# The top-256 selection of a sparse-attention decoder: its number built in float bits, blocks 2 and 3 counted on ScalarE as well

## The chip, the cores and the metric

The kernel runs on one core of a Trainium2 chip. Its time is the device time of one launch in microseconds (us). Four engines compute, each with its own queue worked off in order: TensorE (PE in the profile; PEld is its weight load), VectorE (DVE), ScalarE (ACT) and GpSimd (POOL); SyncE (SP) issues the DMAs. They meet only at semaphores.

## The reference

Two layers of a decoder over 1024 tokens of 1024 features. The first mixer is a sparse attention in which an indexer scores every earlier key for every query and the 256 best keys are kept; the second is a sliding-window attention. Each layer also reads a small memory and ends in a gated MLP with a causal convolution. The part that matters here:

```python
dots  = jnp.einsum('bqhd,bsd->bqhs', qi, k_idx)               # 16 index heads
score = jnp.einsum('bqhs,bqh->bqs', relu(dots), wi)
score = jnp.where(causal[None], score, -jnp.inf)
_, idx = lax.top_k(score, 256)                                # per query, of up to 1024 keys
# softmax attention of 8 heads over the keys in idx alone
```

## The kernel before

Activations lie with the features on the partitions and 512 tokens (a half) in a row. A product in float32 is made of three passes in the reduced-precision format (`mm3`, lines 256 to 258): every operand is split into a high part, which ACT casts, and a rest, which POOL or DVE subtracts. Weights are split ahead of their use (cast on line 99, ACT; rest on line 100, POOL; two units ahead), products are evacuated from PSUM by ACT and then DVE (lines 264 and 265). PSUM has two buffers `pS` of 1024 columns and four `pB` of 512.

The queries are worked in blocks of 128. Block b has (b + 1) * 128 keys. `indexer` makes the scores: for each of 16 heads PE multiplies into one or two `pB` (line 1188), ACT takes the relu of each piece (line 1191), and DVE adds head by head into the block's `work` tile (line 1194 for the first head, 1196 for the others). `topk` then finds the 256th largest score of every row, for several blocks at once: 32 steps, one for each bit of a float32. In each step every block is counted against its candidate `cand`: a block on DVE by a comparison with an accumulator (line 1224, tile `hit`), a block in the argument `act` by a Sign pass with an accumulator on ACT (line 1232, tile `sign`). Small DVE instructions on tiles of 128x2 or 128x4 (lines 1229, 1246, 1249 to 1253) keep or drop the bit and make the next candidate. Blocks on ACT are refined at the end by four passes over the row and a fresh count (lines 1263 to 1272), since a Sign pass counts ties by half. Masks follow (lines 1280 to 1290).

The order of each queue is that in which the program issues, and that is set by `tick`: PE's work in the foreground calls it with an estimate in ns, and background generators (the indexer, `topk`, norms, the memory's attention) run as far as that budget goes. A `yield` names what a step costs, so `pace` (1400 ns a count for blocks 2 and 3, 2400 ns for blocks 4 to 7) spaces the counts. In the program of `index`, blocks 2 and 3 are scored, then selected, while blocks 4 to 7 are scored; then blocks 4 to 7 are selected, with blocks 6 and 7 on ACT, through the attention and the first MLP.

Of the kernel before, what the change touches and what calls it, by code (L numbers as in the profile page):

```python
# [17 lines left out]
F32 = mybir.dt.float32  # L18
R32 = mybir.dt.float32r
I32 = mybir.dt.int32  # L20
BF16 = mybir.dt.bfloat16
AF = mybir.ActivationFunctionType
OP = mybir.AluOpType
# [7 lines left out]
TOPK = 256  # L31
# [142 lines left out]
class Trunk:  # L174
# [1028 lines left out]
    def topk(self, blks, pace, act=()):  # L1203

        nc, nb = self.nc, len(blks)
        wks = [self.work[b][:, :(b + 1) * 128] for b in blks]
        ints = self.sb.tile([128, 6, 4], I32, name="ti", tag="ti", bufs=2)
        found, flip, cand, keep, less, pick = [ints[:, i, :nb] for i in range(6)]
        floats = self.sb.tile([128, 5, 4], F32, name="tc", tag="tc", bufs=2)
        cnt, need, reach, low, high = [floats[:, i, :nb] for i in range(5)]
        order = [i for i in range(nb) if blks[i] not in act]
        order[1:1] = [i for i in range(nb) if blks[i] in act]

        def hits(tag):  # L1220
            return self.sb.tile([128, 1024], BF16, name=tag, tag=tag, bufs=1)

        def count(i, op):
            nc.vector.tensor_scalar(hits("hit")[:, :(blks[i] + 1) * 128], wks[i], cand[:, i:i + 1].bitcast(F32), 0.0,
                                    op0=op, op1=OP.add, accum_out=cnt[:, i:i + 1])

        def counts():
            if act:
                nc.vector.tensor_scalar(less, cand, -(1 << 31), None, op0=OP.bitwise_xor)
            for i in order:  # L1230
                if blks[i] in act:
                    nc.scalar.activation(hits("sign")[:, :(blks[i] + 1) * 128], wks[i], AF.Sign,
                                         bias=less[:, i:i + 1].bitcast(F32), accum_out=cnt[:, i:i + 1])
                else:
                    count(i, OP.is_ge)
                yield pace

        for i, b in enumerate(blks):
            nc.vector.memset(need[:, i:i + 1], float(2 * TOPK - 1 - (b + 1) * 128 if b in act else TOPK))
        nc.vector.memset(found, 0)  # L1240
        nc.vector.memset(cand, 0)
        yield from counts()
        nc.vector.tensor_tensor(reach, cnt, need, op=OP.is_lt)
        nc.vector.tensor_scalar(flip, reach, -1.0, 0.0, op0=OP.mult, op1=OP.add)
        for bit in range(30, -1, -1):
            nc.vector.scalar_tensor_tensor(cand, found, 1 << bit, flip, op0=OP.bitwise_or, op1=OP.bitwise_xor)
            yield from counts()
            if act:
                nc.vector.tensor_tensor(reach, cnt, need, op=OP.is_ge)
                nc.vector.tensor_scalar(keep, reach, float(1 << bit), 0.0, op0=OP.mult, op1=OP.add)  # L1250
            else:
                nc.vector.tensor_scalar(keep, cnt, float(TOPK), float(1 << bit), op0=OP.is_ge, op1=OP.mult)
            nc.vector.tensor_tensor(found, found, keep, op=OP.bitwise_or)
        nc.vector.tensor_tensor(cand, found, flip, op=OP.bitwise_xor)
        for i in range(nb):
            count(i, OP.is_gt)
            yield pace
        for i, (b, wk) in enumerate(zip(blks, wks)):
            if b in act:
                c = cand[:, i:i + 1]  # L1260
                far = self.t4(1024)[:, :(b + 1) * 128]
                for end, side, away, near in ((low, OP.is_le, 3.4e38, OP.min), (high, OP.is_gt, -3.4e38, OP.max)):
                    nc.vector.tensor_scalar(far, wk, c.bitcast(F32), away, op0=side, op1=OP.mult)
                    yield 1.6 * (b + 1) * 128
                    nc.vector.tensor_tensor_reduce(far, far, wk, 1.0, away, op0=OP.add, op1=near,
                                                   accum_out=end[:, i:i + 1])
                    yield 1.6 * (b + 1) * 128
                lo, hi, p = low[:, i:i + 1].bitcast(I32), high[:, i:i + 1].bitcast(I32), pick[:, i:i + 1]
                nc.vector.tensor_scalar(p, cnt[:, i:i + 1], float(TOPK), -1.0, op0=OP.is_ge, op1=OP.mult)
                nc.vector.tensor_tensor(c, lo, hi, op=OP.bitwise_xor)  # L1270
                nc.vector.tensor_tensor(c, c, p, op=OP.bitwise_and)
                nc.vector.tensor_tensor(c, c, hi, op=OP.bitwise_xor)
                yield 1.6 * (b + 1) * 128
                count(i, OP.is_gt)
                yield 1.6 * (b + 1) * 128
        nc.vector.tensor_scalar(cnt, cnt, -1.0, float(TOPK), op0=OP.mult, op1=OP.add)
        for i, wk in enumerate(wks):
            n = (blks[i] + 1) * 128
            eq, rank = self.t4(1024)[:, :n], self.t4(1024)[:, :n]
            v = cand[:, i:i + 1].bitcast(F32)  # L1280
            nc.vector.tensor_scalar(eq, wk, v, 1.0, op0=OP.is_equal, op1=OP.mult)
            yield 0.8 * n
            nc.vector.tensor_tensor_scan(rank, eq, eq, 0.0, op0=OP.add, op1=OP.max)
            yield 2 * 0.8 * n
            nc.vector.scalar_tensor_tensor(rank, rank, cnt[:, i:i + 1], eq, op0=OP.is_le, op1=OP.mult)
            yield 2 * 0.8 * n
            nc.vector.scalar_tensor_tensor(wk, wk, v, rank, op0=OP.is_le, op1=OP.subtract)
            yield 2 * 0.8 * n
            nc.vector.tensor_scalar(wk, wk, NEG, 1.0, op0=OP.mult, op1=OP.mult)
            yield 0.8 * n  # L1290
# [395 lines left out]
    def run(self):  # L1686
        nc, a = self.nc, self.a
# [52 lines left out]
        def memory():  # L1740
            yield from self.mem_norm()
            yield from self.mem_kv(0)
            del self.mn
# [6 lines left out]
        def index():  # L1750
            yield 12864
            yield from self.indexer((2, 3))
            bt.append(self.add_bg(self.topk((2, 3), 1400)))
            while "qi1" not in self.marks:
                yield 500
            yield 9000
            be[1] = 0.65
            yield from self.indexer((4, 5, 6, 7))
            late.append(self.add_bg(self.topk((4, 5, 6, 7), 2400, (6, 7))))

        late = []
        bt = []
        be = self.add_bg(index(), 1.0)
        self.finish_bg(b1)
        del x1
# [29 lines left out]
        for hf in range(2):  # L1795
# [8 lines left out]
            if hf == 0:  # L1804
# [14 lines left out]
                bm, bt = self.add_bg(memory()), []  # L1819
            else:  # L1820
# [9 lines left out]
                def mem_kv():  # L1830
                    yield 120000
                    yield from self.mem_norm()
                    yield 3000
                    yield from self.mem_kv(1)
                    del self.mn

                bt = [self.add_bg(mem_kv(), 0.8)]
# [289 lines left out]
```

## Time and profile before

| | |
|---|---|
| median of 3 runs (2682.31 to 2684.56) | 2682.89 us |
| the profiled execution | 2683.7 us |
| its span, first to last instruction | 2681.9 us |
| mean granted PE clock | 0.965 |
| busy: PE, DVE, POOL, ACT | 92%, 66%, 50%, 44% |
| selection of blocks 2 and 3: first count and end of the last step | 184.5 and 357.8 us |
| selection of blocks 4 to 7: first and last Sign pass | 401.4 and 797.8 us |

PE is the busiest engine, and what it does is the same before and after; time moves where PE waits, or where its granted clock falls, which in the records is 1.2 GHz instead of 2.4 for some us after a wait. The two selections run in the stretch from 184 to 860 us, so that is the stretch to read, engine by engine.

### The profile page before, as it was taken

To read this page: it belongs to the slowest core of one execution; us is meant where nothing else is said; L and a number is where in the kernel's file an instruction comes from. 1 tells how busy PE (TensorE), PEld (TensorE's weight loads), DVE (VectorE), ACT (ScalarE), POOL (GpSimd) and SP (SyncE) were. 2 spreads that over 40 slices of the span, in tenths; PEclk is the share of its full clock that TensorE was granted. 3 is DMA by queue.
4 is the path that set the end of the run, shared out by engine and by line. 5 is a ranking of instruction groups with operands and counts; after the bars stand their busy time and mean duration, and the time that the engine had idled before them with its cause. 6 is when DMAs were issued, how large, how long until landed. Compare 5 with 4: busy or idle time off the path is not lost. (4 is left out here: it accounts for less than half of the span.)

```text
span 2681.9 us, 33704 instructions
## 1 busy us (share of the span) xinstructions
PE 2480.3 (92%) x11912; PEld 2066.6 (77%) x11912; DVE 1775.3 (66%) x3016; ACT 1190.1 (44%) x2214; POOL 1344.5 (50%) x942
## 2 busy tenths in 40 slices
PE   6789889988998999989999989999989999999997
PEld 5667667867776789877778878878867888887886
DVE  7899997876679556664663361588786565655446
ACT  4444456644442555433333333678744444442103
POOL 4544343444554643336756555656645666664203
PEclk8899999998998999999999999999999999999998
DMA  5444345422222254232323327453144323249301
GB/s 198 145 150 133 127 135 209 148 72 88 84 85 74 77 201 126 87 118 79 104 84 110 102 75 235 136 187 115 67 157 157 120 101 124 97 145 365 134 24 63
DMA packets 122233, 338.00 MB, mean 126 GB/s; under 512 B 13136, under 2 KB 30032, under 8 KB 122064
## 3 DMA queue, kind: packets, MB, share of 16 engines
q1 hardware_dynamic: 122064, 335.85, 37.4%
q8 instruction: 94, 1.54, 0.2%
q14 instruction: 75, 0.61, 0.1%
HBM read 262.40 MB, written 73.40 MB: 125 GB/s over the span
## 5 line engine op out<-in xcount | busy, mean ns | idle before, releaser
L100 POOL TENSOR_TENSOR t<-t,t 128x1024 fp32r<-128x1024 f32 (+1 forms) x292 | 720.6, 2483 | 483.1 <-ACT t L99 328.9
L256 PE MATMUL pB<-t,t 128*128 128x512 f32 (+3 forms) x1824 | 683.1, 375 | 12.0 <-DVE t L766 4.7
L257 PE MATMUL pB<-t,t 128*128 128x512 f32 (+3 forms) x1824 | 680.3, 373 | 11.6 <-DVE t L447 9.4
L258 PE MATMUL pB<-t,t 128*128 128x512 f32 (+3 forms) x1824 | 680.1, 373 | 8.9 <-POOL t L100 8.9
L256 PE MATMUL pS<-t,t 128*128 128x512 f32 (+1 forms) x1460 | 578.7, 396 | 59.5 <-DVE t L852 28.0
L258 PE MATMUL pS<-t,t 128*128 128x512 f32 (+1 forms) x1460 | 572.7, 392 | 13.1 <-POOL t L100 13.1
L257 PE MATMUL pS<-t,t 128*128 128x512 f32 (+1 forms) x1460 | 572.6, 392 | 0.8 <-DVE t L498 0.8
L256 PEld LDWEIGHTS pB<-t,t 128*128 128x128 f32 (+1 forms) x1824 | 347.0, 190 | 73.3 <-DVE t L766 5.0
L257 PEld LDWEIGHTS pB<-t,t 128*128 128x128 f32 (+1 forms) x1824 | 347.0, 190 | 71.9 <-DVE t L447 10.7
L258 PEld LDWEIGHTS pB<-t,t 128*128 128x128 f32 (+1 forms) x1824 | 346.9, 190 | 71.0 <-POOL t L100 10.8
L256 PEld LDWEIGHTS pS<-t,t 128*128 128x128 f32 x1460 | 284.1, 195 | 122.1 <-DVE t L852 37.7
L99 ACT CAST t<-t 128x1024 fp32r<-128x1024 f32 (+1 forms) x292 | 296.9, 1043 | 101.8 <-PE pS L258 44.4
L258 PEld LDWEIGHTS pS<-t,t 128*128 128x128 f32 x1460 | 283.3, 194 | 74.1 <-POOL t L100 17.5
L257 PEld LDWEIGHTS pS<-t,t 128*128 128x128 f32 x1460 | 284.0, 195 | 53.0 <-DVE t L498 1.6
L106 POOL TENSOR_TENSOR t<-t,t 128x512 fp32r<-128x512 f32 x133 | 177.4, 1347 | 136.9 <-ACT t L105 136.9
L265 DVE TENSOR_TENSOR t<-pB,t 128x512 fp32r<-128x512 f32 (+3 forms) x248 | 149.8, 623 | 84.3 <-ACT t L264 81.8
L264 ACT CAST t<-pB 128x512 fp32r<-128x512 f32 (+3 forms) x248 | 126.5, 535 | 151.8 <-PE pB L258 82.5
L1040 DVE TENSOR_TENSOR t<-t,pS 128x1024 f32<-128x1024 f32 (+1 forms) x92 | 108.0, 1174 | 124.0 <-PE pS L258 123.8
L796 POOL TENSOR_TENSOR t<-t,t 128x512 f32<-128x512 f32 x44 | 57.2, 1299 | 201.8 <-ACT t L795 201.8
L852 DVE TENSOR_TENSOR t<-t,pS 128x1024 f32<-128x1024 f32 x88 | 106.5, 1217 | 65.2 <-PE pS L258 65.0
L1415 POOL TENSOR_SCALAR t<-t,st 128x128 f32<-128x128 f32 (+3 forms) x64 | 47.9, 751 | 141.6 <-DVE st L1414 78.9
L787 ACT ACTIVATE t<-t,conv 128x512 f32<-128x512 f32 x44 | 35.9, 816 | 175.8 <-DVE t L786 175.8
(239 smaller groups left out, 3405.3 us busy)
## 6 DMA issues: line engine op xcount, KB each, us to landing
t<-in_up SPq DMA_DIRECT2D x138, 512.0 KB
t<-in_down SPq DMA_DIRECT2D x66, 512.0 KB
G_d<-t SPq DMA_DIRECT2D x44, 512.0 KB
t<-G_d SPq DMA_DIRECT2D x44, 512.0 KB
t<-in_a_in SPq DMA_DIRECT2D x42, 512.0 KB
t<-in_b_in SPq DMA_DIRECT2D x28, 512.0 KB
t<-in_a_out SPq DMA_DIRECT2D x20, 512.0 KB
t<-x_d SPq DMA_DIRECT2D x20, 512.0 KB
```

Of the source, the lines that this page charges most:

```text
L99: nc.scalar.copy(hi[:, :w], raw[:, :w])
L100: nc.gpsimd.tensor_tensor(lo[:, :w], raw[:, :w], hi[:, :w].bitcast(F32), op=OP.subtract)
L106: nc.gpsimd.tensor_tensor(hl[:, 1], src, hl[:, 0].bitcast(F32), op=OP.subtract)
L256: mm(out, a[0], b[0], start=start, stop=False, skip_group_check=again)
L257: mm(out, a[0], b[1], start=False, stop=False, skip_group_check=again)
L258: mm(out, a[1], b[0], start=False, stop=stop, skip_group_check=again)
L264: nc.scalar.copy(hi, src)
L265: nc.vector.tensor_tensor(lo, src, hi.bitcast(F32), op=OP.subtract)
L796: nc.gpsimd.tensor_tensor(v, v, rb[0], op=OP.mult)
L852: nc.vector.tensor_tensor(x[dp][:, :, t], x[dp][:, :, t], S, op=OP.add)
L1040: nc.vector.tensor_tensor(xp, xp, S, op=OP.add)
L1415: nc.gpsimd.tensor_scalar(Pt[:, :n], Pt[:, :n], st[:, 2:3], 1.0, op0=OP.mult, op1=OP.mult)
```

## The change

In `topk` the blocks are put in a new order, those counted on DVE (`own`) first. `cand` is now itself the number that is built: a step makes `drop`, the bit if too few scores reach the candidate, and takes it back and sets the next bit with one exclusive-or instruction. That is two small instructions for each group of blocks in a step, where there were three (no block on ACT) or five. For the group on ACT the number is kept with its sign bit turned over, so that it serves as the bias of the Sign pass. All Sign passes of a step have one width, that of the widest block; the narrower blocks' tiles are filled up by a memset on POOL. The Sign passes are issued first in a step, right behind the decision of the step before, and the `yield` for them comes behind the DVE counts. Blocks 2 and 3 are now both in `act`: they have no DVE count in the 32 steps, and are refined at the end as blocks 6 and 7 are.

```diff
--- before.py
+++ after.py
@@ -1208,14 +1208,19 @@
 
 
+
+
         nc, nb = self.nc, len(blks)
+        own = [b for b in blks if b not in act]
+        blks = own + [b for b in blks if b in act]
         wks = [self.work[b][:, :(b + 1) * 128] for b in blks]
-        ints = self.sb.tile([128, 6, 4], I32, name="ti", tag="ti", bufs=2)
-        found, flip, cand, keep, less, pick = [ints[:, i, :nb] for i in range(6)]
-        floats = self.sb.tile([128, 5, 4], F32, name="tc", tag="tc", bufs=2)
-        cnt, need, reach, low, high = [floats[:, i, :nb] for i in range(5)]
-        order = [i for i in range(nb) if blks[i] not in act]
-        order[1:1] = [i for i in range(nb) if blks[i] in act]
+        ints = self.sb.tile([128, 3, 4], I32, name="ti", tag="ti", bufs=2)
+        cand, drop, pick = [ints[:, i, :nb] for i in range(3)]
+        floats = self.sb.tile([128, 3, 4], F32, name="tc", tag="tc", bufs=2)
+        cnt, low, high = [floats[:, i, :nb] for i in range(3)]
+        wide = (max(act) + 1) * 128 if act else 0
+        parts = [(slice(0, len(own)), TOPK), (slice(len(own), nb), 2 * TOPK - 1 - wide)]
+        parts = [p for p in parts if p[0].stop > p[0].start]
 
         def hits(tag):
             return self.sb.tile([128, 1024], BF16, name=tag, tag=tag, bufs=1)
@@ -1224,34 +1229,29 @@
             nc.vector.tensor_scalar(hits("hit")[:, :(blks[i] + 1) * 128], wks[i], cand[:, i:i + 1].bitcast(F32), 0.0,
                                     op0=op, op1=OP.add, accum_out=cnt[:, i:i + 1])
 
-        def counts():
+        nc.vector.memset(cand, 0)
+        if act:
+            nc.vector.tensor_scalar(cand[:, len(own):], cand[:, len(own):], -(1 << 31), None, op0=OP.bitwise_xor)
+            for b in act:
+                if (b + 1) * 128 < wide:
+                    nc.gpsimd.memset(self.work[b][:, (b + 1) * 128:wide], -3e38)
+        for bit in range(31, -1, -1):
+            for b in act:
+                i = blks.index(b)
+                nc.scalar.activation(hits("sign")[:, :wide], self.work[b][:, :wide], AF.Sign,
+                                     bias=cand[:, i:i + 1].bitcast(F32), accum_out=cnt[:, i:i + 1])
+            for i in range(len(own)):
+                count(i, OP.is_ge)
+                yield pace
             if act:
-                nc.vector.tensor_scalar(less, cand, -(1 << 31), None, op0=OP.bitwise_xor)
-            for i in order:
-                if blks[i] in act:
-                    nc.scalar.activation(hits("sign")[:, :(blks[i] + 1) * 128], wks[i], AF.Sign,
-                                         bias=less[:, i:i + 1].bitcast(F32), accum_out=cnt[:, i:i + 1])
-                else:
-                    count(i, OP.is_ge)
-                yield pace
-
-        for i, b in enumerate(blks):
-            nc.vector.memset(need[:, i:i + 1], float(2 * TOPK - 1 - (b + 1) * 128 if b in act else TOPK))
-        nc.vector.memset(found, 0)
-        nc.vector.memset(cand, 0)
-        yield from counts()
-        nc.vector.tensor_tensor(reach, cnt, need, op=OP.is_lt)
-        nc.vector.tensor_scalar(flip, reach, -1.0, 0.0, op0=OP.mult, op1=OP.add)
-        for bit in range(30, -1, -1):
-            nc.vector.scalar_tensor_tensor(cand, found, 1 << bit, flip, op0=OP.bitwise_or, op1=OP.bitwise_xor)
-            yield from counts()
-            if act:
-                nc.vector.tensor_tensor(reach, cnt, need, op=OP.is_ge)
-                nc.vector.tensor_scalar(keep, reach, float(1 << bit), 0.0, op0=OP.mult, op1=OP.add)
-            else:
-                nc.vector.tensor_scalar(keep, cnt, float(TOPK), float(1 << bit), op0=OP.is_ge, op1=OP.mult)
-            nc.vector.tensor_tensor(found, found, keep, op=OP.bitwise_or)
-        nc.vector.tensor_tensor(cand, found, flip, op=OP.bitwise_xor)
+                yield pace * len(act)
+            for at, need in parts:
+                nc.vector.tensor_scalar(drop[:, at], cnt[:, at], float(need), float(1 << bit) if bit < 31 else -1.0,
+                                        op0=OP.is_lt, op1=OP.mult)
+                nc.vector.scalar_tensor_tensor(cand[:, at], drop[:, at], 1 << bit >> 1, cand[:, at],
+                                               op0=OP.bitwise_xor, op1=OP.bitwise_xor)
+        if act:
+            nc.vector.tensor_scalar(cand[:, len(own):], cand[:, len(own):], -(1 << 31), None, op0=OP.bitwise_xor)
         for i in range(nb):
             count(i, OP.is_gt)
             yield pace
@@ -1750,7 +1750,7 @@
         def index():
             yield 12864
             yield from self.indexer((2, 3))
-            bt.append(self.add_bg(self.topk((2, 3), 1400)))
+            bt.append(self.add_bg(self.topk((2, 3), 1400, (2, 3))))
             while "qi1" not in self.marks:
                 yield 500
             yield 9000
```

PE's and SP's queues hold the same instructions in the same order as before. Three places where the others differ:

First, ACT's queue where the selection of blocks 2 and 3 begins. L1191 with 128x512 are the last relus of block 3, L264 an evacuation, L466 the high part of the normed second half. Before:

```order
L1191 ACTIVATE t_1446<-pB 128x512
L1191 ACTIVATE t_1463<-pB 128x512
L1191 ACTIVATE t_1469<-pB 128x512
L264 CAST t_1493<-pS 128x1024
L99 CAST t_1500<-t_1207 128x1024
L466 CAST t_1510<-t_1386 128x1024
L466 CAST t_1514<-t_1455 128x1024
L99 CAST t_1522<-t_1333 128x1024
```

and with the change, where the line of the Sign pass is L1241:

```order
L1191 ACTIVATE t_1446<-pB 128x512
L1191 ACTIVATE t_1463<-pB 128x512
L1191 ACTIVATE t_1469<-pB 128x512
L1241 ACTIVATE sign,tc<-t_1110,ti 128x512
L1241 ACTIVATE sign,tc<-t_1297,ti 128x512
L264 CAST t_1494<-pS 128x1024
L99 CAST t_1501<-t_1207 128x1024
L466 CAST t_1511<-t_1386 128x1024
L466 CAST t_1515<-t_1455 128x1024
L99 CAST t_1523<-t_1333 128x1024
```

The first two Sign passes stand ahead of L264, L99 and both L466; they wait for the first `cand`, which is DVE's row behind L1200 of block 3.

Second, one step in the scoring of block 6 (pieces of 512 and 256 columns): ACT before, two heads and a weight cast,

```order
L1191 ACTIVATE t_2295<-pB 128x512
L1191 ACTIVATE t_2295<-pB 128x256
L1191 ACTIVATE t_2317<-pB 128x512
L1191 ACTIVATE t_2317<-pB 128x256
L99 CAST t_2328<-t_2037 128x1024
L1191 ACTIVATE t_2344<-pB 128x512
```

ACT with the change, the same heads,

```order
L1191 ACTIVATE t_2280<-pB 128x512
L1191 ACTIVATE t_2280<-pB 128x256
L1191 ACTIVATE t_2300<-pB 128x512
L1191 ACTIVATE t_2300<-pB 128x256
L1241 ACTIVATE sign,tc<-t_1110,ti 128x512
L1241 ACTIVATE sign,tc<-t_1297,ti 128x512
L99 CAST t_2312<-t_2025 128x1024
L1191 ACTIVATE t_2328<-pB 128x512
```

and DVE with the change, where L1249 and L1251 are the decision:

```order
L1196 SCALAR_TENSOR_TENSOR t_2251<-t_2280,wtok,t_2251 128x768
L1196 SCALAR_TENSOR_TENSOR t_2251<-t_2300,wtok,t_2251 128x768
L1249 TENSOR_SCALAR ti<-tc 128x2
L1251 SCALAR_TENSOR_TENSOR ti<-ti 128x2
L1196 SCALAR_TENSOR_TENSOR t_2251<-t_2328,wtok,t_2251 128x768
L1196 SCALAR_TENSOR_TENSOR t_2251<-t_2344,wtok,t_2251 128x768
L1249 TENSOR_SCALAR ti<-tc 128x2
```

The decision stands behind the second head's L1196, and the Sign passes stand between that head's relu and whatever ACT does next. Before, the same place of DVE's queue held, for these heads:

```order
L1196 SCALAR_TENSOR_TENSOR t_2267<-t_2317,wtok,t_2267 128x768
L1252 TENSOR_SCALAR ti<-tc 128x2
L1253 TENSOR_TENSOR ti<-ti 128x2
L1246 SCALAR_TENSOR_TENSOR ti<-ti 128x2
L1224 TENSOR_SCALAR hit,tc<-t_1110,ti 128x384
L1196 SCALAR_TENSOR_TENSOR t_2267<-t_2344,wtok,t_2267 128x768
L1224 TENSOR_SCALAR hit,tc<-t_1297,ti 128x512
L1196 SCALAR_TENSOR_TENSOR t_2267<-t_2362,wtok,t_2267 128x768
L1252 TENSOR_SCALAR ti<-tc 128x2
```

Third, ACT in the attention, where L1412 are the exponentials. Before, the Sign passes of blocks 6 and 7 are apart:

```order
L1232 ACTIVATE sign,tc<-t_2654,ti 128x896
L264 CAST t_4808<-pB 128x384
L1412 ACTIVATE t_4760,st<-t_4760,st 128x384
L1412 ACTIVATE t_4791,st<-t_4791,st 128x512
L264 CAST t_4829<-pB 128x384
L1232 ACTIVATE sign,tc<-t_3120,ti 128x1024
```

With the change they are neighbours:

```order
L1241 ACTIVATE sign,tc<-t_2630,ti 128x1024
L1241 ACTIVATE sign,tc<-t_3088,ti 128x1024
L1412 ACTIVATE t_4009,st<-t_4009,st 128x128
L1412 ACTIVATE t_4037,st<-t_4037,st 128x256
L264 CAST t_4080<-pB 128x512
L264 CAST t_4016<-pB 128x512
```

Here both have 1024 columns.

## Rows read from the trace of the kernel before

**Rows 1.** Page, part 1 and one row of part 5: busy, mean ns; idle before, releaser.
```profile
PE 2480.3 (92%) x11912; PEld 2066.6 (77%) x11912; DVE 1775.3 (66%) x3016; ACT 1190.1 (44%) x2214; POOL 1344.5 (50%) x942
...
L99 ACT CAST t<-t 128x1024 fp32r<-128x1024 f32 (+1 forms) x292 | 296.9, 1043 | 101.8 <-PE pS L258 44.4
```

**Rows 2.** Busy of engines by stretch: PE, PEld, DVE, ACT, POOL, clock, DMA share, GB/s.
```profile
220.50:294.70 74.20, 68.82 (x335) 56.16 (x335) 70.79 (x136) 39.28 (x79) 24.87 (x11) 1.00 0.39 126
294.70:358.00 63.30, 49.81 (x214) 40.91 (x213) 59.33 (x118) 30.02 (x67) 23.31 (x16) 0.89 0.35 117
358.00:400.00 42.00, 37.95 (x170) 29.29 (x168) 40.39 (x42) 25.12 (x49) 19.53 (x12) 0.96 0.40 129
400.00:560.00 160.00, 144.91 (x813) 123.98 (x814) 129.38 (x329) 98.92 (x208) 61.25 (x53) 0.96 0.48 163
560.00:810.00 250.00, 229.76 (x958) 185.99 (x957) 171.64 (x285) 117.52 (x183) 128.33 (x67) 0.95 0.26 83
```

**Rows 3.** Waits of PE, 183 to 400 us: total, times, longest.
```profile
PE pB L1188 <- ACT t L704: 11.7, 3, 8.6
PE pB L257 <- DVE t L447: 7.0, 1, 7.0
```

**Rows 4.** DVE groups, 180 to 360 us.
```profile
L1224 DVE TENSOR_SCALAR_CACHE_REDUCE hit<-t,ti 128x512 bf16<-128x512 f32 x33 | 24.4, 741 | 0.3
L1224 DVE TENSOR_SCALAR_CACHE_REDUCE hit<-t,ti 128x384 bf16<-128x384 f32 x33 | 20.2, 613 | 1.2
L1252 DVE TENSOR_SCALAR ti<-tc 128x2 int32<-128x2 f32 x31 | 17.9, 578 | 0.2
```

**Rows 5.** ACT groups, 400 to 810 us: the sign passes.
```profile
L1232 ACT ACTIVATE sign<-t,ti 128x1024 bf16<-128x1024 f32 x32 | 36.7, 1148 | 0.5
L1232 ACT ACTIVATE sign<-t,ti 128x896 bf16<-128x896 f32 x32 | 33.3, 1040 | 54.0 <-DVE ti L1229 53.9
L1232 ACT ACTIVATION_READ_ACCUMULATOR sign<-t,ti 128x1 f32 x64 | 12.0, 188 | 0.0
```

**Rows 6.** Timeline, 257 to 261 us: start, us, instruction.
```profile
257.55 2.52 POOL L100 TENSOR_TENSOR t<-t,t 128x1024 fp32r<-128x1024 f32 x1 [1.90 <-PE pB L1188]
...
257.72 2.37 DVE L1252 TENSOR_SCALAR ti<-tc 128x2 int32<-128x2 f32 x1
```

**Rows 7.** Timeline, 267 to 275 us: one bit, its heads and its decision.
```profile
267.45 1.62 ACT L1191 ACTIVATE t<-pB 128x512 f32<-128x512 f32 x4
...
270.56 0.86 PE L1188 MATMUL pB<-t,t 128*128 128x512 f32 x4
...
272.65 0.86 PE L1188 MATMUL pB<-t,t 128*128 128x512 f32 x4
...
272.71 1.02 DVE L1196 SCALAR_TENSOR_TENSOR t<-t,wtok,t 128x768 f32<-128x768 f32 x1
273.64 0.16 DVE L1252 TENSOR_SCALAR ti<-tc 128x2 int32<-128x2 f32 x1
...
274.03 0.16 DVE L1246 SCALAR_TENSOR_TENSOR ti<-ti 128x2 int32<-128x2 int32 x1
```

**Rows 8.** Timeline, 173 to 188 us: where the selection of blocks 2 and 3 begins.
```profile
173.89 1.02 ACT L264 CAST t<-pS 128x1024 fp32r<-128x1024 f32 x1 [2.08 <-PE pS L258]
...
182.13 2.32 DVE L1200 TENSOR_TENSOR t<-t,tri 128x128 f32<-128x128 f32 x1
...
187.80 0.58 PE L257 MATMUL pB<-t,t 128*128 128x256 f32 x1 [7.03 <-DVE t L447]
```

**Rows 9.** Line 1232: what its engine waited for, us and times.
```profile
  DVE ti L1229: 53.9, 17
```

**Rows 10.** Waits of PE, 560 to 810 us.
```profile
PE pS L256 <- DVE t L852: 16.7, 6, 6.0
```

**Rows 11.** DVE groups, 806 to 860 us: refinement of blocks 6 and 7.
```profile
L1263 DVE TENSOR_SCALAR t<-t,ti 128x896 f32<-128x896 f32 x2 | 3.1, 1566 | 0.0
L1265 DVE CUSTOM_DVE_ANT_0 t<-t,t 128x896 f32<-128x896 f32 x2 | 4.2, 2120 | 0.0
```

## The prediction

> **What bounds the kernel now.** I read the page's busy table first: PE is busy 92% of the span, DVE 66%, ACT 44% [rows 1]. So the end moves only by what PE waits for, and PE's list of instructions is the same after the change. Then the table of stretches [rows 2], for the time of both selections. It shows what the shares of the whole span hide: from 220.5 to 294.7 us, where blocks 4 to 6 are scored and blocks 2 and 3 selected, DVE is busy 70.8 of 74.2 us, ACT 39.3 and PE 68.8. Up to 358 us DVE has 59.3 of 63.3 and up to 400 us 40.4 of 42.0; there PE falls to 49.8 of 63.3 and its clock to 0.89. The waits of PE say why: 7.0 us for line 447 on DVE, and 11.7 us for line 704 on ACT [rows 3], whose inputs come from DVE. DVE is behind, and that shows on PE late in the stretch. From 400 us on DVE is busy 129.4 of 160 us and 171.6 of 250.
>
> **The change, part by part, by the profiled execution of 2683.7 us.**
>
> *DVE's relief.* Of 33 counts at each width 32 go: 32 x (741 + 613) ns = 43 us [rows 4], and with them one small instruction of three in each step, 32 x 0.2 us = 6 us [rows 7]. That is nearly 50 us of DVE between 184 and 358 us. It is worth nothing by itself; it counts if what PE waits for next comes sooner.
>
> *ACT's new step.* The Sign pass at 512 columns is not in the trace; 1024 and 896 columns take 1148 and 1040 ns [rows 5], so 512 is an estimate of 1040 - 3 x 108 = 716 ns, plus 188 ns for the accumulator read, less 0.1 us of overlap: 0.8 us, two of them 1.6 us. More weighs where they stand. In the new order a step is, on ACT, relu, relu, Sign, Sign; and the Sign pass waits for `cand`, which DVE makes after the second head's L1196. Take two heads of block 6 [rows 7]: both relus need 1.62 us. The first head's sum starts at 0.85 us; the sums are 0.93 us apart (272.71 to 273.64), so the second ends at 2.7 us; two small instructions at 0.2 us each end at 3.1 us. ACT has waited 1.5 us. With the Sign passes the step takes 4.75 us. PE needs 2 x 2.09 us for these heads and the products between them (270.56 to 272.65). ACT works in order, so behind a waiting Sign pass stand the next relus, which free `pB` for PE's L1188, and the weight casts of line 99. ACT with its waits becomes the slowest loop of this stretch.
>
> From 220.5 to 294.7 us there are 32 heads, and 16 steps in the new order: 16 x 4.75 = 76 us, less 3 us since half of the heads are narrower. To this come 8 casts of line 99 at 1.04 us [rows 1] and 7 other instructions of about the same size: 15 us, together 88 us. A cast sets off line 100 on POOL, and a small DVE instruction or an L1196 that starts while it runs ends with it: L1252 took 2.37 us at 257.72 beside POOL's 2.52 us at 257.55, and 0.16 us alone [rows 6, 7]. Behind 8 casts that adds up to 1.5 us each, so 100 us. I take the middle, 94: **20 us more** than 74.2 (14 to 26).
>
> The Trainium skill has a rule for this, in "SBUF — State Buffer", Who interferes with whom: VectorE and GpSimd share a pair of ports under an exclusive lock, taken by a tensor_scalar or by an instruction with two SBUF inputs, but not by the tensor_scalar that also writes its accumulator. The trace agrees: the counts stay at 613 and 741 ns on average, L1252 has a mean of 578 for 0.16 us of work [rows 4]. So the change takes from DVE the instructions that POOL never held up, and puts those that it does hold up between ACT and its next pass. By the rule alone, each of the 8 casts blocks, and the stretch is 100 us; without it 88.
>
> *The end of that stretch, 294.7 to 358 us.* 8 steps with heads of block 7, some 0.25 us longer, are 40 us, less 3 for steps with one head, 3 for heads behind the last step, 14 for ACT's other work (its 30.0 less some 16 pairs of relus of about 1 us), and up to 5 for blocking: 59 us against 63.3, since DVE's lag no longer delays line 704. **4 us less** (12 less to 4 more).
>
> *The beginning.* The first two Sign passes stand ahead of L264, L99 and both L466 and wait for DVE's row behind L1200 of block 3, at 182.13; L264 ran at 173.89 [rows 8]. ACT is shut for some 9 us. L264, L99 and two L466 follow from about 184.5, then line 447, for which PE already waits until 187.80. **4 us more** (0 to 8).
>
> *Refinement of blocks 2 and 3, new, between 358 and 400 us.* 8 passes, 8 small instructions and two counts on a DVE that has 1.6 us free there. At 896 columns the passes took 1566 and 2120 ns [rows 11]; at half the width I take 0.5 to 1.5 us, so 10 us of DVE with the small ones. Some is covered, as DVE comes without its lag: **6 us more** (0 to 12).
>
> *Blocks 4 to 7, 400 to 560 us.* Four small instructions for five, but the Sign passes follow the decision at once. Before, with one pace of 2400 ns between, ACT already waited 53.9 us in 17 places [rows 9]. Now a step shuts ACT for the wait and 2.3 us of two passes together, while the attention fills four `pB`. PE is busy 144.9 of 160 us here, so there is little to win. About ten steps of 0.6 us: **6 us more** (2 less to 20 more).
>
> *560 to 810 us.* DVE saves a small instruction of 0.2 to 2.4 us in each of some 18 steps and no longer waits for a Sign pass; ACT is shut longer, and line 787 behind it. PE waits 16.7 us for L852 [rows 10], which is also what can be won. **0** (17 less to 12 more). The 128 columns more in block 6 cost ACT 32 x 0.1 us, covered by its idle half.
>
> Sum: 20 - 4 + 4 + 6 + 6 + 0 = 32 us, 2715.7; the median of the runs lies 0.8 us under the profiled execution, so **2715 us**.
>
> **The rivals.** *DVE's lag was all there was* (faster). If Sign passes mostly find `cand` ready, because relus come at PE's pace and other casts fill the gap, DVE's 50 us go to PE: the 18.7 us of [rows 3] and the half-speed share of 63.3 x 0.11 + 42.0 x 0.04 = 9 us, up to 28, less the refinement's 6: 2662. For it speaks 95% of DVE; against it the order, where a relu, its sum, the decision and the Sign pass are one chain with nothing between. It decides if ACT's wait stays under 0.4 us a step, since 1.62 + 1.6 + 0.95 of casts is PE's 4.18. *It cancels*: lag won equals chain lost, 2684. *Attention suffers too*: the two neighbouring passes and the wait keep ACT away some 5 us, and PE, four `pB` ahead, loses 2 us in each of ten steps instead of 0.6, with all blocking: 2715 + 14 for those waits + 6 for blocking + 10 for a clock that falls with them, as it cost 7 us (0.11 x 63.3) before 358 us, makes 2745. *The change does not do what it says* only in this: the steps of blocks 4 to 7 have four small instructions, not two.
>
> **How the numbers follow.** The forecast has 0.57, the faster case 0.18, cancelling 0.10, the bad attention 0.15. A difference under 0.2% can't be told from none here. Slower: 0.57 + 0.15 = 0.72; same 0.10; faster 0.18. The forecast's own range is 2698 to 2735; that for 8 in 10 goes halfway into the outer cases, 2668 to 2758.
>
> **What would show it.** DVE's busy falls by some 45 us and ACT's rises by 55. ACT's wait for the decision (new line 1251) is the largest of ACT's list, over 60 us, some 1.5 us each in the scoring; PE's wait for L1191 grows from a few us to over 20, and that for line 704 shrinks. From the first relu of block 4 to the end of block 6's scoring, 32 heads take 88 to 100 us. The prediction is wrong if these 32 heads take 80 us or less, or if PE's waits there name DVE as before.

## The result, and the profile after

The changed kernel takes 2728.81 us (median of 4 runs, 2724.2 to 2729.45), the kernel before 2683.72 us beside it; the ratio is 1.0164, with a 95% interval of 1.0147 to 1.018. It is slower, by 45 us, where 32 were forecast. The profiled execution of after took 2728.98 us, its span 2727.1, its mean granted clock 0.96.

The busy row of the page, to be held against [rows 1]:

```profile
PE 2499.9 (92%) x11912; PEld 2080.4 (76%) x11912; DVE 1697.9 (62%) x2845; ACT 1242.2 (46%) x2342; POOL 1339.4 (49%) x944
```

DVE lost 77 us of busy time and ACT gained 52, and that is no help: PE runs the same 11912 matmuls and was busy 20 us longer with them.

Since PE's list is the same in all kernels here, one can take the k-th matmul of each trace and subtract the times. Such differences from the trace of before are the measure below ("33.5 us behind at 294.9" is the matmul that before starts at 294.9). Busy of engines by stretch for after, the same pieces of PE's list as [rows 2] within a microsecond (start to end, length, PE, PEld, DVE, ACT, POOL, clock, DMA share, GB/s):

```profile
227.90:328.40 100.50, 79.97 (x336) 63.70 (x335) 58.25 (x87) 59.38 (x134) 23.98 (x10) 0.88 0.33 107
328.40:397.10 68.70, 53.04 (x213) 41.08 (x212) 39.20 (x57) 43.61 (x104) 20.99 (x16) 0.93 0.27 87
397.10:441.10 44.00, 37.43 (x171) 29.94 (x169) 42.72 (x60) 23.90 (x47) 16.22 (x12) 0.92 0.39 123
441.10:624.70 183.60, 152.93 (x813) 129.04 (x814) 128.45 (x318) 103.93 (x212) 63.16 (x54) 0.92 0.42 142
624.70:856.70 232.00, 223.81 (x958) 183.16 (x957) 141.98 (x262) 118.90 (x182) 128.65 (x67) 0.97 0.27 89
```

By their columns, (b + 1) * 128, the 32 heads of the first stretch are those of blocks 4 and 5, and the second stretch scores block 6: the 768 columns of [rows 7], and of the step shown under the change, are block 5's. What stands ahead of here numbers these blocks one too high; its sums go by heads and rows and are not touched by that. The scoring of blocks 4 and 5 grew by 26 us, the attention by 24, and the MLP shrank by 18. In the scoring no engine is full now: DVE fell from 70.8 of 74.2 us to 58.3 of 100.5, ACT has 59.4. That is the picture of a chain of waits. They stand in the waits of PE and ACT from 228 to 397 us:

```profile
PE pB L1188 <- ACT t L1191: 15.5, 10, 3.6
PE pB L698 <- ACT t L1191: 7.7, 3, 3.3
PE pB L1188 <- ACT t L704: 6.9, 3, 3.1
```

```profile
ACT sign L1241 <- DVE ti L1251: 48.0, 20, 4.2
ACT t L1191 <- PE pB L1188: 9.5, 8, 2.7
ACT sign L1241 <- DVE st L707: 7.2, 2, 4.3
```

PE's wait for line 704 shrank from the 11.7 us of [rows 3], and the relu of line 1191 took its place. ACT waits 2.4 us each time for the decision. DVE waited for no Sign pass in this window. One step from the timeline, in block 5 as [rows 7] is (start, us, instruction, in brackets the wait and what ended it):

```profile
288.02 0.72 ACT L1241 ACTIVATE sign<-t,ti 128x512 bf16<-128x512 f32 x1 [1.78 <-DVE ti L1251]
...
289.59 1.03 ACT L99 CAST t<-t 128x1024 fp32r<-128x1024 f32 x1
290.53 1.62 ACT L1191 ACTIVATE t<-pB 128x512 f32<-128x512 f32 x4
290.70 2.40 POOL L100 TENSOR_TENSOR t<-t,t 128x1024 fp32r<-128x1024 f32 x1 [9.55 <-ACT t L99]
291.42 3.61 DVE L1196 SCALAR_TENSOR_TENSOR t<-t,wtok,t 128x768 f32<-128x768 f32 x2 [3.49 <-ACT t L1191]
294.94 0.16 DVE L1249 TENSOR_SCALAR ti<-tc 128x2 int32<-128x2 f32 x1
295.14 0.16 DVE L1251 SCALAR_TENSOR_TENSOR ti<-ti 128x2 int32<-128x2 int32 x1
295.40 0.72 ACT L1241 ACTIVATE sign<-t,ti 128x512 bf16<-128x512 f32 x1 [3.25 <-DVE ti L1251]
297.59 1.01 PE L1188 MATMUL pB<-t,t 128*128 128x512 f32 x4 [1.95 <-ACT t L1191]
```

The relus end at 292.15, the sums only at 295.03, since the first of them stands beside POOL's line 100 (3.61 us for two, where [rows 7] has 1.02 for one); then the decision, then the passes, and only behind them the relus that free `pB` for PE. From Sign pass to Sign pass it is 7.4 us (288.02 to 295.40), for two heads that cost PE 4.2.

In the attention PE, DVE and ACT wait like this with the change, 441.1 to 624.7 us:

```profile
PE pB L1432 <- DVE t L265: 7.2, 4, 3.8
PE pB L256 <- DVE t L265: 6.9, 4, 4.1
PE pB L1402 <- DVE t L265: 6.0, 1, 6.0
```

```profile
DVE t L265 <- ACT t L264: 27.5, 27, 3.2
```

```profile
ACT sign L1241 <- DVE ti L1251: 23.4, 10, 5.5
```

and in the same piece before, 400.7 to 560.4 us:

```profile
DVE t L265 <- ACT t L264: 12.4, 16, 2.7
```

```profile
ACT sign L1232 <- DVE ti L1229: 14.5, 5, 5.9
```

Line 264 is the evacuation on ACT, line 265 its other half on DVE. ACT waits for the decision twice as often, DVE then for ACT, and PE for DVE: before, PE waited 3.5 us for L1402 and 1.0 for L256 there.

### The profile page after: what moved, and what is told of

It is laid out like the page before. It is cut to its first block, busy times and chain, and to the rows that moved or that the text cites. A ratio compares the mean times of both kernels' runs of the same rounds, so it can differ in the third digit from the quotient of the medians.

```text
span 2727.1 us, 33641 instructions
## 1 busy us (share of the span) xinstructions
PE 2499.9 (92%) x11912; PEld 2080.4 (76%) x11912; DVE 1697.9 (62%) x2845; ACT 1242.2 (46%) x2342; POOL 1339.4 (49%) x944
## 5 line engine op out<-in xcount | busy, mean ns | idle before, releaser
L256 PE MATMUL pB<-t,t 128*128 128x512 f32 (+3 forms) x1824 | 686.2, 376 | 20.8 <-DVE t L265 6.9
L256 PE MATMUL pS<-t,t 128*128 128x512 f32 (+1 forms) x1460 | 581.1, 398 | 50.0 <-ACT t L99 20.3
L256 PEld LDWEIGHTS pB<-t,t 128*128 128x128 f32 (+1 forms) x1824 | 349.3, 191 | 84.1 <-DVE t L265 8.1
L256 PEld LDWEIGHTS pS<-t,t 128*128 128x128 f32 x1460 | 285.8, 196 | 112.0 <-DVE t L852 24.0
L99 ACT CAST t<-t 128x1024 fp32r<-128x1024 f32 (+1 forms) x292 | 296.9, 1043 | 101.5 <-PE pS L258 44.4
L264 ACT CAST t<-pB 128x512 fp32r<-128x512 f32 (+3 forms) x248 | 125.6, 534 | 158.5 <-PE pB L258 85.8
L1241 ACT ACTIVATE sign<-t,ti 128x512 bf16<-128x512 f32 (+1 forms) x128 | 119.6, 935 | 143.1 <-DVE ti L1251 115.9
L1196 DVE SCALAR_TENSOR_TENSOR t<-t,wtok,t 128x384 f32<-128x384 f32 (+5 forms) x90 | 116.3, 1293 | 61.4 <-ACT t L1191 56.6
L852 DVE TENSOR_TENSOR t<-t,pS 128x1024 f32<-128x1024 f32 x88 | 106.8, 1217 | 67.9 <-PE pS L258 67.8
```

The lines of the kernel that those rows point to most:

```text
L99: nc.scalar.copy(hi[:, :w], raw[:, :w])
L256: mm(out, a[0], b[0], start=start, stop=False, skip_group_check=again)
L264: nc.scalar.copy(hi, src)
L852: nc.vector.tensor_tensor(x[dp][:, :, t], x[dp][:, :, t], S, op=OP.add)
L1196: nc.vector.scalar_tensor_tensor(work[:, :n], tmp[:, :n], wv, work[:, :n], op0=OP.mult, op1=OP.add)
L1241: nc.scalar.activation(hits("sign")[:, :wide], self.work[b][:, :wide], AF.Sign, bias=cand[:, i:i + 1].bitcast(F32), accum_out=cnt[:, i:i + 1])
```

## The experiments

Theory 1 says that a Sign pass right behind the decision it needs makes ACT wait in order, and that this wait is the cost. Its rivals are the load of the passes on ACT, and the new number with its order. How far each kernel is behind before (us; negative is ahead) at five matmuls of before, by the profiled executions (three pairs of these kernels have the same code in this part: after and steps of 4 to 7 apart, one pace later and both repairs, the two with blocks 2 and 3 on DVE; up to 358.0 they differ by at most 0.9 us, so at least that much is noise):

| kernel | 220.6 | 294.9 | 358.0 | 560.4 | 810.1 | median us | ratio, 95% interval |
|---|---|---|---|---|---|---|---|
| after | 7.3 | 33.5 | 39.1 | 64.3 | 46.6 | 2728.81 | 1.0147 to 1.018 |
| blocks 2, 3 on DVE | -0.4 | -2.8 | -4.5 | 17.1 | -2.3 | 2683.34 | 0.999 to 1.0008 |
| old number, 2, 3 on ACT | 6.2 | 34.4 | 38.2 | 45.5 | 45.6 | 2729.85 | 1.0159 to 1.019 |
| passes one pace later | 2.1 | 11.0 | 2.5 | 31.5 | 10.8 | 2693.09 | 1.0025 to 1.0055 |
| passes that wait for nothing | 0.4 | -6.5 | -22.2 | 2.7 | -19.6 | 2663.36 | 0.9911 to 0.9944 |
| no passes for 2, 3 | 2.3 | -4.5 | -22.1 | 5.1 | -15.2 | 2667.55 | 0.993 to 0.9962 |
| steps of 4 to 7 apart | 8.2 | 34.4 | 40.0 | 44.5 | 35.3 | 2718.9 | 1.0117 to 1.0153 |
| both repairs | 1.9 | 10.8 | 2.2 | 6.9 | -10.2 | 2674.32 | 0.9961 to 0.9981 |
| 2, 3 on DVE, steps apart | -0.1 | -2.5 | -4.2 | -6.6 | -21.2 | 2662.43 | 0.9915 to 0.994 |
| 2 and 3 in turns | 2.8 | 4.7 | -6.1 | 0.3 | -14.2 | 2667.13 | 0.9932 to 0.9957 |
| 2 on DVE, 3 on ACT | 0.2 | 2.0 | -10.1 | -9.2 | -25.7 | 2655.87 | 0.9882 to 0.9915 |

**Blocks 2 and 3 on DVE again** (from after):

```diff
-            bt.append(self.add_bg(self.topk((2, 3), 1400, (2, 3))))
+            bt.append(self.add_bg(self.topk((2, 3), 1400)))
```

> After's kernel with blocks 2 and 3 counted on VectorE again; the number building in raw bits and the neighbouring Sign passes of blocks 4 to 7 stay. Theory 1 (in the scoring the chain relu, L1191's consumer L1196, decision, Sign pass is the cost): the +39 us up to 358 us go, with the refinement; the +24 us of 400 to 560 and the -18 us of 560 to 810 stay: 2683 + 6 = about 2690 us (2680 to 2700). Rival (the number building or the order of its instructions is what costs in the scoring too): about 2729 us. DVE's wait for L1191's relu goes from 31.5 us back to a few.

2683.34 us, no difference from before. The 39 us went, so the rival falls; and with two small instructions in place of three the kernel is 6 us ahead by 400 us, which the forecast of 2690 had left out. DVE's wait for the relu is down to 3.5 us, 4 times. The attention still loses 23 us and the MLP gives 19 back: with the 6 us, all three cancel.

**The old number, with blocks 2 and 3 on ACT** (the same line changed the other way, in before):

> Before's kernel, its five small instructions a bit and Sign passes one pace apart, with only this edit: blocks 2 and 3 are counted on ScalarE. Theory 1 (the wait of ScalarE for VectorE's decision costs, whatever the number is built with): slower than before by the +39 us of the scoring, the refinement, and a bit for three more small instructions in each chain, while 400 to 810 us is as before: about 2725 to 2740 us. Rival (ScalarE's counting itself is harmless, the new number's order costs): about 2685 to 2695 us.

2729.85 us. The losses up to 358 us are those of after within 1.1 us at each column, though the number is built in the old way. ACT's wait for the decision from 227 to 396 us:

```profile
ACT sign L1232 <- DVE ti L1229: 55.1, 20, 4.5
```

Between 358 and 400 us, with the refinement, it loses 5 us more, where after lost 1.3. From there its steps are before's, and the difference is 45.5 us at 560 and 45.6 at 810. The two experiments are each other's mirror: the place of blocks 2 and 3 alone makes the 39 us, the new steps of blocks 4 to 7 alone the +24 and -18.

**The passes one pace behind the decision** (from after):

```diff
         for bit in range(31, -1, -1):
+            if not own:
+                yield pace
             for b in act:
...
-                yield pace * len(act)
+                yield pace * (len(act) if own else 1)
```

> After's kernel; for blocks 2 and 3 one of the two paces of a step is put between the decision and the Sign passes, so that they are issued a head later than the decision; the number of instructions and the length of a step are the same. Theory 1 (ScalarE stands and waits because the passes come right behind the decision): most of the waits of L1241 for the decision go and 10 to 25 of the 39 us with them: about 2710 us (2700 to 2720). Rival 2 (ScalarE's added load of 1.6 us a step is the cost, its waits only take the place of others): 2729 us as after.

2693.09 us: 36 of the 45 us are gone with nothing left out, more than forecast, and the rival falls: the load is the same. ACT still waits, less often; 222.7 to 360.5 us:

```profile
ACT sign L1243 <- DVE ti L1253: 23.9, 14, 3.2
```

What is left is of this kind (timeline, 269 to 273 us), with a DVE instruction held up ahead of the passes: of the 13 waits over 0.7 us twelve stand behind one, ten behind a sum of line 1196 and two, as this one, behind the decision itself:

```profile
269.35 1.05 ACT L99 CAST t<-t 128x1024 fp32r<-128x1024 f32 x1
...
270.48 2.41 POOL L100 TENSOR_TENSOR t<-t,t 128x1024 fp32r<-128x1024 f32 x1 [5.35 <-ACT t L99]
270.62 2.28 DVE L1253 SCALAR_TENSOR_TENSOR ti<-ti 128x2 int32<-128x2 int32 x1
...
273.00 0.72 ACT L1243 ACTIVATE sign<-t,ti 128x512 bf16<-128x512 f32 x1 [1.83 <-DVE ti L1253]
```

The decision's second instruction is 0.16 us of work; it begins beside POOL's line 100 and ends with it at 272.9. This is the rule that the prediction cites from the Trainium skill, "SBUF — State Buffer", Who interferes with whom (an instruction with two SBUF inputs contends with a GpSimd read, and whichever issues first holds the other up), and the row agrees.

**Passes that wait for nothing** (from after; the bias and the accumulator of blocks 2 and 3 are other tiles; not shown: the memsets of these tiles, of `cnt` and, at the end, of `cand`):

```diff
-                                     bias=cand[:, i:i + 1].bitcast(F32), accum_out=cnt[:, i:i + 1])
+                                     bias=(cand if own else still)[:, i:i + 1].bitcast(F32), accum_out=(cnt if own else gone)[:, i:i + 1])
```

> After's kernel, but the Sign passes of blocks 2 and 3 read a constant column as their bias and write a column that nobody reads, so they wait for no decision: the same passes at the same place on ScalarE, the same small instructions on VectorE (the selection of these two blocks is left out by that). Theory 1 (the wait for the decision is the cost): 25 to 40 us less than after, 2690 to 2704 us, and L1241 waits for nothing in the scoring. Rival 2 (the load of the passes on ScalarE is the cost): 2720 to 2729 us.

2663.36 us, beyond the expected end. From 221 us on no Sign pass waits. The same passes stand at the same place in ACT's queue, and PE is 22 us ahead of before at 358 us in place of 39 behind: the wait is worth 61 us. Its stretches, the first two of after's table:

```profile
221.00:288.40 67.40, 67.40 (x335) 56.60 (x334) 56.02 (x84) 59.93 (x138) 23.92 (x10) 1.00 0.49 153
288.40:335.80 47.40, 46.23 (x213) 37.94 (x213) 38.51 (x55) 41.31 (x100) 24.20 (x15) 1.00 0.41 136
```

PE has no idle time in the first and 1.2 us in the second; ACT's 59.9 us of work fit under it. So theory 1 put the wait too small: DVE's relief is real, 22 us, and the chain hides it besides costing 39.

**No passes at all** (from after; not shown: the same memsets of `cnt` and `cand`):

```diff
-            for b in act:
+            for b in act if own else ():
```

> After's kernel without the Sign passes of blocks 2 and 3 (their selection is left out by that): VectorE has the relief and the small instructions, ScalarE has no added load. The free Sign passes left PE 22 us ahead of before at 358 us. Theory 1 (ScalarE's load costs nothing there as long as it waits for nobody): about the same as with free passes, 2655 to 2665 us. Rival 2 (the load costs too): 2640 to 2652 us.

2667.55 us, 2.5 above the expected range and with an interval that overlaps that of the free passes; both are 22 us ahead at 358. The 64 passes of 0.9 us (58 us of ACT) cost nothing as long as they wait for nobody. So the load on ACT is no cause by itself; what it adds where passes do wait is the question of the last two kernels.

**Blocks 4 to 7 in steps one pace apart, new number kept** (from after; the call's arguments are not shown):

```diff
-            for b in act:
-                i = blks.index(b)
-                nc.scalar.activation(...)
-            for i in range(len(own)):
-                count(i, OP.is_ge)
-                yield pace
-            if act:
+            order = list(range(len(own)))
+            order[1:1] = range(len(own), nb)
+            for i in order:
+                if i < len(own):
+                    count(i, OP.is_ge)
+                    yield pace
+                else:
+                    nc.scalar.activation(...)
+                    if own:
+                        yield pace
+            if not own:
                 yield pace * len(act)
```

> After's kernel with the steps of blocks 4 to 7 in the old order (count of block 4, Sign pass, Sign pass, count of block 5, one pace between any two), the number still in raw bits with four small instructions. Theory 1 (the two Sign passes side by side, right behind the decision, cost the +24 us of 400 to 560 us and bring the -18 us of 560 to 810 us): both go, 2729 - 24 + 18 = about 2723 us, and PE's difference from before stays level from 400 to 810 us. Rival (the small instructions bring the -18 us, the order costs the +24): 2705 us. Rival (the small instructions and the width of 1024 cost the +24 us): 2729 us or up to 2747.

2718.9 us, between theory 1's 2723 and the first rival's 2705. The attention is settled: from 400.7 to 560.4 it loses 1.6 us (42.9 to 44.5) in place of 24. DVE's wait at the evacuation, 443.6 to 604.8 us, is nearly back at before's 12.4:

```profile
DVE t L265 <- ACT t L264: 15.2, 17, 3.4
```

Of the MLP's 18 us, 9 stay with the steps apart and come with the number, and 9 need the neighbouring passes. The DVE groups that make a decision show what changes, in the same piece of the MLP: before (560.4 to 810.1 us), apart (604.8 to 845.4), after (624.7 to 856.7); busy us, mean ns, idle before:

```profile
L1250 DVE TENSOR_SCALAR ti<-tc 128x4 int32<-128x4 f32 x22 | 17.6, 799 | 0.8
L1249 DVE TENSOR_TENSOR tc<-tc 128x4 f32<-128x4 f32 x22 | 13.9, 633 | 6.8 <-ACT sign L1232 6.2
...
L1253 DVE TENSOR_TENSOR ti<-ti 128x4 int32<-128x4 int32 x22 | 9.9, 451 | 0.8
...
L1246 DVE SCALAR_TENSOR_TENSOR ti<-ti 128x4 int32<-128x4 int32 x21 | 6.6, 316 | 0.7
L1229 DVE TENSOR_SCALAR ti<-ti 128x4 int32<-128x4 int32 x21 | 5.7, 270 | 0.7
```

```profile
L1255 DVE SCALAR_TENSOR_TENSOR ti<-ti 128x2 int32<-128x2 int32 x44 | 30.3, 689 | 1.5
...
L1253 DVE TENSOR_SCALAR ti<-tc 128x2 int32<-128x2 f32 x44 | 21.5, 490 | 0.4
```

```profile
L1249 DVE TENSOR_SCALAR ti<-tc 128x2 int32<-128x2 f32 x44 | 13.4, 304 | 0.0
L1251 DVE SCALAR_TENSOR_TENSOR ti<-ti 128x2 int32<-128x2 int32 x44 | 11.4, 258 | 1.5
```

With the passes side by side these instructions fall less often beside POOL's work: 25 us, in place of 52 with the steps apart and 54 before. Each of them that took over 0.3 us, 23 before, 23 with the steps apart and 6 in after, began while one of POOL's lines 100, 796 and 806 ran, and ended within 0.03 us of its end. PE's wait for L852, 16.7 us in [rows 10], is 10.6 with the steps apart and 6.5 in after. Why the decision lands at a quieter place was not tried, so that half of the gain stays unexplained.

**Both repairs**: blocks 2 and 3 one pace later as above, and blocks 4 to 7 apart in the attention only (from the kernel with the steps apart; the paces, which follow `mid`, are not shown):

```diff
+            mid = 1 if bit > 17 else 0
-            order[1:1] = range(len(own), nb)
+            order[mid:mid] = range(len(own), nb)
```

> Both repairs in after's kernel: blocks 2 and 3 keep ScalarE, with one of the two paces between the decision and the Sign passes; blocks 4 to 7 take the steps one pace apart for the 14 bits that fall into the attention (31 to 18), and the neighbouring Sign passes from bit 17 on. Theory 1 (the places add up): 2.5 us behind before at 358 us, 6 at 400, 2 more to 560, 18 back to 810: 2683 + 8 - 18 = about 2673 us. Rival (the MLP's 18 us come only because the attention left the selection late, so that they go with the 24): about 2691 us.

2674.32 us against 2673: the places add up to about that, and the MLP's gain does not hang on the attention's loss.

**Blocks 2 and 3 on DVE, steps of 4 to 7 as in both repairs** (`topk((2, 3), 1400)`):

> The same steps for blocks 4 to 7, but blocks 2 and 3 counted on VectorE as before the change, with the new number. Theory 1: 6 us ahead of before at 400 us, level to 560, 19 us back to 810: 2683 - 6 + 2 - 18 = about 2660 us. Rival as above: 2678 us. If 2660 comes, the raw-bit number alone, with other places for the passes, is worth more than the work on ScalarE.

2662.43 us against 2660. Faster than before by 0.7% without a pass more on ACT, and 12 us faster than both repairs, which differ from it only in counting blocks 2 and 3 on ACT.

**Blocks 2 and 3 in turns**, both on ACT (from both repairs; `sign` and `decide` hold the pass and the two small instructions; the rest is not shown):

```diff
+        for t in range(0 if own else 32 * nb + 1):
+            if t:
+                i = (t - 1) % nb
+                decide(31 - (t - 1) // nb, slice(i, i + 1), parts[0][1])
+            if t < 32 * nb:
+                sign(t % nb)
+                yield pace
```

> As the kernel with both repairs, but blocks 2 and 3 take turns: at each pace one block's decision and the other block's Sign pass, one pace after its own decision, so that ScalarE has one pass of 0.9 us a head in place of two in every second head; VectorE has 64 more small instructions of 0.16 us or more. Theory 1 (a burst of two passes behind a late decision is what is left of the loss): 5 to 10 us less than the kernel with both repairs, 2663 to 2668 us. Rival (what is left comes from decisions held up beside GpSimd's part of a weight cast, 2.28 us for 0.16, and these become twice as many): the same 2673 us or up to 10 more.

2667.13 us, and 8 us better than both repairs at 358 us. So the burst of two passes was part of what still cost: though the decisions are twice as many, PE loses less. It stays 5 us slower than with both blocks on DVE.

**One block on each engine**: count of block 2, one pace, Sign pass of block 3, one pace, decision (from both repairs):

```diff
-            mid = 1 if bit > 17 else 0
+            mid = 1 if bit > 17 or nb == 2 else 0
...
-            bt.append(self.add_bg(self.topk((2, 3), 1400, (2, 3))))
+            bt.append(self.add_bg(self.topk((2, 3), 1400, (3,))))
```

> The kernel with both repairs, but block 2 is counted on VectorE and only block 3 on ScalarE, in the order count, one pace, Sign pass, one pace, decision: one pass of 0.9 us a step, and half of VectorE's relief. Free passes left PE 22 us ahead of before at 358 us, counting on VectorE 4, taking turns 6. Theory 1 (what matters is that a pass finds its decision made): at 358 us 6 to 16 us ahead, refinement of one block 2 back, then as the other kernels with steps apart: 2650 to 2662 us. Rival (VectorE must lose both counts for the relief to show, and any pass behind a late decision costs): 2662 to 2670 us, no better than counting both on VectorE.

2655.87 us (2655.09 to 2657.72), ratio 0.9899, interval 0.9882 to 0.9915: the fastest of all, 1% under before and 2.7% under after. ACT's and PE's waits from 220.8 to 348 us:

```profile
ACT sign L1249 <- DVE ti L1260: 30.0, 16, 4.0
```

```profile
PE pB L1188 <- ACT t L1191: 8.2, 5, 2.8
PE pB L1188 <- ACT t L704: 2.0, 1, 2.0
```

ACT waits more than where both blocks come one pace later (30.0 us against 23.9), and PE less (10.4 against 14.4 in all). So the sum of ACT's waits is not the price. The room in its loop may be: in a step that waits, ACT needs 1.6 us of relus, 0.9 for the one pass and 1.9 of wait (30.0 / 16), 4.4 us against PE's 4.2; one pace later it was 1.6 + 1.8 + 1.7 = 5.1, and in after 1.6 + 1.8 + 2.4 = 5.8. That is an estimate from these rows, without casts; it puts the three kernels in the order of their times at 358 us, and no run shows it by itself.

## Why the prediction was right, and where not

The direction, the main mechanism and the range held; the forecast of 2715 us was 14 short. By its own steps:

- **DVE's relief worth nothing by itself**: it holds as it was put, on the condition that PE's next input must come sooner. With passes that wait PE is 39 us behind at 358 us; with passes that wait for nothing, or with none, it is 22 ahead. The faster rival priced that at 2662 us, and the kernel that never waits came out at 2663.4 (there, too, attention and MLP cancel, +22 and -22). Its condition, a wait under 0.4 us a step, does not come out of its sum, 4.17 of PE's 4.18 us, which leaves 0.01; ACT waited 2.4.
- **Scoring, +20 (14 to 26)**: +26, at the range's end; the 32 heads took 100.5 us, where 88 to 100 were named. The chain was the one described. What was too small is the share of holding up: 94 was the middle between none of it and all of it, 100, and all of it came. In that stretch eight sums of line 1196 took 2.46 to 2.82 us in place of 0.89 and 1.02, 12.7 us in all, seven of them beside line 100 and one beside POOL's line 555; and ACT's wait was 2.4 us, not 1.5. It was the sums: the decision's second instruction, 15 times, took 0.161 us on average.
- **The end of that stretch, -4 (-12 to +4)**: +5.6, the wrong sign and past the range. The step put eight waits of 1.5 us, 12 in all, and up to 5 for holding up. The Sign passes waited 23.2 us there (16.0 in 7 for L1251, and 7.2 in 2 that the profile puts down to DVE's line 707).
- **The beginning, +4 (0 to 8)**: +7.3, in the range and at another place. ACT was shut for 9.0 us as forecast, but at before's 200 us after was level again (PE waits 5.0 us for a cast of line 99 in place of 7.0 for line 447). The loss came between 200 and 210, where PE waited 2.2 us for line 99 and 2.0 for line 100 behind waiting passes, and where its clock fell: up to 220 it was busy 36.4 us, at 0.87, for what it does in 33.5, at 0.92, with blocks 2 and 3 on DVE. Free passes are 0.4 behind at 220, so the loss is the wait's.
- **Refinement, +6 (0 to 12)**: +1.3 in after, and 5 with the old number.
- **Attention, +6 (-2 to +20)**: +24, outside its range and the most mis-sized term. The cause was named (two neighbouring passes and the wait shut ACT), and ten waits came, but 0.6 us was put in for each where ACT waited 2.3 (23.4 in 10), and the clock was left out: PE was busy 152.9 us for matmuls that took it 145.3, at 0.92 instead of 0.96. That is 8 of the 24. The rival that priced it at 2 us a step and a falling clock, 20 us and up to 16 for clock and holding up, came nearer.
- **MLP, 0 (-17 to +12)**: -17.7, just past the end, half with the number and half with the order. "What can be won" was read from [rows 10] as 16.7 us; PE won 10.2 of them, and 6 more by busy time at a clock of 0.97 for 0.95.

The last two errors, +18 and -18, cancel, and that is luck: they have different causes, since both repairs take away the attention's loss and keep the MLP's gain. What lacks in the sum, 44.6 at before's 2600 us against 32, is the other terms: 3.3 + 6.2 + 9.6 - 4.7 = 14.4, less 2 us given back behind 810. Of the signs named ahead, ACT's rise (52 us for 55), its largest wait (115.9 us for L1251 over the span) and PE's wait for the relus (26.6 us at lines 1188, 698 and 413 from 180 to 400 us) came; DVE fell by 77 in place of 45, mostly since the MLP's small instructions lost 29 us of being held up (53.7 to 24.8 us in the rows above).

## What to carry to other kernels

Moving work from a full engine to an idle one can cost more than it frees if it brings a wait into the other's in-order queue: look at what stands between the instruction moved and its input, and put at least one piece of other work there. The Trainium skill ("Perfetto Trace Analysis", Optimizing Scalar/DVE Operations) says that offloading work from a saturated DVE to the scalar engine may make sense. Here it did so only in one of four places, each held against the kernel that counts blocks 2 and 3 on DVE and is otherwise the same: both blocks right behind the decision, 45 us slower (2728.81 against 2683.34); both a pace later, 12 slower (2674.32 against 2662.43); in turns, 5 slower; one block alone, 7 faster, with intervals that meet at 0.9915. The new number with the steps apart in the attention, which moves no work to ACT, gave 20 us. And an edit in shared code is two edits: the same new steps cost 24 us in the attention and gave 18 in the MLP, 9 of these by their order, so choose the order by stage.

## What was not expected of the hardware

- PE's own time for the same matmuls moves with its waits. For the 335 of the scoring it was 67.4 us at a granted clock of 1.00 with no idle time (2.4 GHz throughout), 68.8 in [rows 2], and 80.0 at 0.88 in after, a mean that puts part of the stretch at 1.2 GHz, after waits of 2 to 4 us: its records show 1.2 GHz in five pieces of this stretch, 23.9 us in all, each behind a wait of PE of 2.2 to 3.6 us. Of the 26 us lost there 11 are this.
- Busy time of small DVE instructions can be mostly time held up beside POOL: 44 of one form took 30.3 us in one order and 11.4 in another, for the same 0.16 us of work each.
- 58 us of Sign passes on ACT that wait for nobody did not lengthen the time: 2663.4 us with them, 2667.6 without.
